# The last third of a modulation projection: its 16 weight tiles issued whole in the second mixer's norm

## The chip, the cores and the metric

The kernel runs on one core of one Trainium2 chip. The metric is the device time of one execution in microseconds (us), as the median of several runs.

## The reference

The program computes two blocks, one after the other, in float32. The first has two hybrid layers on 256 tokens of width 1024. A layer is a mixer and a feed-forward:

```
h = rms_norm(x, g_mix);  z = h @ w_in
o_a = mla_mixer(...);  o_b = conv_mixer(...);  o_c = nsa_mixer(...)
x = x + (g_a * o_a + g_b * o_b + g_c * o_c) @ w_out
h = rms_norm(x, g_ffn)
x = x + jnp.square(jax.nn.relu(h @ w_ff1)) @ w_ff2
```

The second block attends from the first one's result, with a context of 256 further tokens. Its norms are modulated: six vectors of 1024 for the tokens and six for the context come from two condition vectors, as `silu(c) @ w_mod + b_mod`, so `w_mod` is 1024 x 6144. Two of its parts are a differential attention and a recurrence over the tokens (wkv, a state of 64 x 64 for each of 16 heads); the recurrence runs over the context first.

## The kernel before, in words

TensorE (PE) does every product. Weights come from HBM by SP's queue, in pieces of up to 512 KB ("raw", four buffers), and each piece is split in two parts, wh by ScalarE (ACT, line 312) and wl by VectorE (DVE, line 277), three buffers each, because a float32 product is made of three passes: lines 333 to 335 or 351 to 353. PE works its instructions in the order in which they were issued, and so does SP's queue. A scheduler fixes that order when the program is built. It goes by the order of the code, by priorities, and by waits on named instructions, so a step that is written elsewhere moves others with it.

In a layer, `mixer` (line 473) norms the tokens, multiplies by w_in in units (tm0 to tm3, then four u2 units for the convolution, and more), runs the three mixers and their merges (oa, ob, oc), and ends with the output projection wo, eight matmul groups of 512 columns. `ffn` (line 888) norms again (`normT`, line 403: squares on ACT, a reciprocal root on DVE, xn scaled by both at lines 415 and 416, 16 transposes on PE at line 424, split into hh and hl at lines 394 and 395) and runs 16 blocks of f1 and f2.

Beside this the program computes pieces of the second block early. `mods_stream` (line 1017) makes the modulation vectors in three thirds of eight units. A unit loads two tiles of 128 x 1024 (line 1034, into one of four buffers named TG) and makes four matmuls of 32 x 512 from them (line 1035, two to a tile). At the end of a third come four transposes (line 1042) and additions. `mods_units(n, after)` (line 1012) issues the next n units; with `after` they are held behind a named matmul, `self.last`, the last of the stage before. The first third and three units of the second are issued in the first layer. The second mixer's norm issues five units, its end three more (before the last part of wo), and the norm of the second feed-forward five.

The four TG buffers also hold the gates that the mixer stored, the first weights of a compression (line 558) and, in `ffn`, constants and a weight for the recurrence (lines 900 to 903 and 1555). In `ffn(1)` the recurrence over the context (`wkv_front`, `wkv_back`) is issued with high priority beside f1 and f2, and its state S is stored at line 907. Its steps are lines 1376 (state times keys), 1392 and 1404 on PE, with VectorE between them. The second block starts by loading S.

Of the kernel before, what the change touches and what calls it, by code (L numbers as in the profile page):

```python
# [194 lines left out]
class Kern:  # L195
# [277 lines left out]
    def mixer(self, l, pool):  # L473
# [11 lines left out]
        hl = self.t(self.work, [128, 8, T], "hl", F32R)  # L485
        self.normT(self.halves(self.x), P["g_mix"], hh, hl, spare="t", hold=True)
        if l:
            self.mods_units(5, self.last)

        if l == 0:  # L490
            nc.sync.dma_start(self.consts, self.A["cst"])
# [253 lines left out]
        with self.stream("n"):  # L745
# [41 lines left out]
            for i0 in range(0, 4, 2):  # L787
# [9 lines left out]
                for j in range(2):  # L797
                    i = i0 + j
# [81 lines left out]
        with self.stream("t"):  # L880
            pw = [self.bank_pair(), [self.score_bank(), self.score_bank()]]
        for i in range(4):
            if i == 3:
                self.mods_units(3)
            self.linB_acc(f"wo{i}_{l}", pw, mh[:, 2 * i:2 * i + 2], ml[:, 2 * i:2 * i + 2], i == 0, i == 3)
        self.add_x(pw)

    def ffn(self, l, pool):

        nc = self.nc  # L890
        hh = self.t(self.work, [128, 8, T], "hh", F32R)
        hl = self.t(self.work, [128, 8, T], "hl", F32R)
        self.normT(self.halves(self.x), self.P["g_ffn"], hh, hl, spare="t")
        self.mods_units(5, self.last)
        self.spare_bank = False
        if l == 0:
            self.ctx_proj(pool)
        with self.stream("n", "c"), self.tc.high_priority(offset=30000):
            self.n4, self.n8 = 5, 6
            tg = self.t(pool, [128, D], "TG", bufs=4)  # L900
            self.wkv_consts(pool, tg[:, T:T + 264])
            wa = tg[:, :T]
            nc.sync.dma_start(wa, self.wad)
            S = self.t(pool, [128, 2, 4, 64], "S")
            nc.gpsimd.memset(S, 0.0)
            self.wkv_back(self.wkv_front(pool, 0, l, self.zc, wa), S)
            nc.sync.dma_start(self.Sd[l], S)
        with self.stream("t"):
            pw = [self.bank_pair(), [self.score_bank(), self.score_bank()]]
        prev = None  # L910
        for i in range(17):
            cur = None
            if i == 14 and l == 0:
                self.mods_units(3)
            if i < 16:
                for ps in self.linA_unit(f"f1{i}_{l}", hh, hl, 8):
                    r = self.t(pool, [128, 2, T], "mt", bufs=4)
                    nc.scalar.activation(r, ps, AF.Relu)
                    fh = self.t(pool, [128, 2, T], "OT", F32R, bufs=2)
                    fl_ = self.t(pool, [128, 2, T], "OL", F32R, bufs=2)  # L920
                    nc.scalar.activation(fh, r, AF.Square)
                    self.mul(r, r, r)
                    self.sub(fl_, r, fh.bitcast(F32))
                    cur = (fh, fl_)
            if i == 15 and l:
                self.ctx_front = [self.t(self.work, [128, 8, T], n, F32R) for n in ("hh", "hl")]
                for n in range(2):
                    nc.sync.dma_start(self.ctx_front[n].bitcast(F32), self.hcd[:, n])
            if prev:
                self.linB_acc(f"f2{i - 1}_{l}", pw, *prev, i == 1, i == 16)  # L930
            prev = cur
        self.spare_bank = True
        self.add_x(pw)
# [1019 lines left out]
```

## Time and profile before

| what | value |
|---|---|
| median of 3 runs | 2797.48 us (2794.47 to 2798.41) |
| the profiled execution | 2798.71 us, its span 2796.9 us |
| mean granted clock of TensorE | 0.946 of full speed |
| busy PE, weight loads, DVE, ACT | 2635.9, 2293.4, 1978.4, 1423.3 us |
| chain that ended last, by engine | PE 79%, DVE 10%, DMA 6%, ACT 4% |

Times of the profile are counted from the span's start. Busy time is the sum of instructions on an engine; the chain is followed back from the last instruction to whatever released each step. A row of a timeline gives the start, the length, the engine, the line, and what is computed from what (`m<-TG,cs` is a PSUM tile m from the weights TG and the condition cs), how many equal ones follow each other, and in brackets the idle time before it with what ended it. The records of a matmul overlap with the next one's, so prices are read from starts. Most tiles give four records; a few are missing.

### The profile page before, as it was taken

Reading aid. Unit: us, or ns where it says so; the run is one execution under the profiler, and the core shown is the slowest. Engines: PE = TensorE matmul, PEld = TensorE weight load, DVE = VectorE, ACT = ScalarE, POOL = GpSimd, SP = SyncE. Lnnn points to the kernel's source line nnn. Section 1 sums busy time; section 2 is a strip of 40 time slices with the busy share of each in tenths; the row PEclk is TensorE's granted clock in tenths of the full one; section 3 lists DMA queues with packets and bytes.
Section 4 is the critical chain, followed back from the end, with each engine's and each line's share of the span. In section 5 each row is a group of like instructions: output and inputs, shape, how many; then the busy total and the mean of one; then the engine's idle time right before and its main releaser. Section 6 shows DMA issues by size and latency. Waiting matters only on the chain.

```text
span 2796.9 us, 54976 instructions
## 1 busy us (share of the span) xinstructions
PE 2635.9 (94%) x21856; PEld 2293.4 (82%) x21856; DVE 1978.4 (71%) x4085; ACT 1423.3 (51%) x2392; POOL 14.2 (1%) x45
## 2 busy tenths in 40 slices
PE   7999899999999999987998979989989999999999
PEld 7986588886997768877888755779989998888887
DVE  5996668765897658766788776566987765666665
ACT  4554446543555446534664655444446554444444
POOL 0000000000000000000000000000000000000000
PEclk9999999999999999988999976699999999999999
DMA  5532866546543555535746522264664346666665
GB/s 189 175 124 88 263 225 199 168 152 219 167 147 126 162 199 170 173 107 166 237 134 200 166 68 59 67 200 163 190 185 137 122 149 208 215 208 219 207 216 183
DMA packets 212433, 472.00 MB, mean 169 GB/s; under 512 B 52816, under 2 KB 86480, under 8 KB 211152
## 3 DMA queue, kind: packets, MB, share of 16 engines
q1 hardware_dynamic: 212176, 468.48, 52.4%
q8 instruction: 172, 2.82, 0.4%
q14 instruction: 85, 0.70, 0.1%
HBM read 427.77 MB, written 40.63 MB: 167 GB/s over the span
## 4 chain that ended last, share of the span: by engine, by line
PE 79%; DVE 10%; DMA 6%; ACT 4%; issue 2%; SPq 0%; DVEq 0%; ACTq 0%
PE a L333 8%; PE a L335 8%; PE a L334 8%; PE b L353 4%; PE b L351 4%; PE b L352 4%; PE b L1767 3%; PE x L335 3%; PE x L333 3%; PE x L334 3%; PE a L352 3%; PE a L351 3%; PE a L353 3%; DVE wl L277 3%; DMA raw<-in_peer 2%
## 5 line engine op out<-in xcount | busy, mean ns | idle before, releaser
L312 ACT ACTIVATE wh<-raw 128x1024 fp32r<-128x1024 f32 (+1 forms) x701 | 638.2, 913 | 689.3 <-PE a L334 247.4
L277 DVE TENSOR_TENSOR wl<-raw,wh 128x1024 fp32r<-128x1024 f32 (+1 forms) x701 | 727.4, 1041 | 357.9 <-ACT wh L312 332.6
L333 PE MATMUL a<-hh,wh 128*128 128x256 f32 x1920 | 550.2, 287 | 8.8 <-ACT hh L1621 4.1
L335 PE MATMUL a<-hh,wl 128*128 128x256 f32 x1920 | 549.5, 286 | 4.5 <-DVE wl L277 4.2
L334 PE MATMUL a<-hl,wh 128*128 128x256 f32 x1920 | 547.2, 285 | 0.6 <-DVE hl L277 0.5
L333 PEld LDWEIGHTS a<-hh,wh 128*128 128x128 f32 x1920 | 365.5, 190 | 22.0 <-ACT wh L312 4.9
L335 PEld LDWEIGHTS a<-hh,wl 128*128 128x128 f32 x1920 | 365.2, 190 | 14.8 <-DVE wl L277 9.0
L334 PEld LDWEIGHTS a<-hl,wh 128*128 128x128 f32 x1920 | 364.9, 190 | 5.4 <-DVE hl L277 0.7
L333 PE MATMUL x<-hh,wh 128*128 128x256 f32 x720 | 205.8, 286 | 5.6 <-ACT wh L312 5.2
L335 PE MATMUL x<-hh,wl 128*128 128x256 f32 x720 | 206.6, 287 | 3.0 <-DVE wl L277 3.0
L334 PE MATMUL x<-hl,wh 128*128 128x256 f32 x720 | 204.9, 285 | 0.0
L352 PE MATMUL b<-wl,ah 128*128 128x512 f32 x512 | 201.0, 393 | 0.0
L351 PE MATMUL b<-wh,ah 128*128 128x512 f32 x512 | 191.2, 393 | 2.8 <-issue 2.8
L353 PE MATMUL b<-wh,al 128*128 128x512 f32 x512 | 191.8, 391 | 0.0
L333 PEld LDWEIGHTS x<-hh,wh 128*128 128x128 f32 x720 | 137.2, 191 | 9.0 <-ACT wh L312 6.7
L335 PEld LDWEIGHTS x<-hh,wl 128*128 128x128 f32 x720 | 136.9, 190 | 5.7 <-DVE wl L277 4.4
L1802 ACT ACTIVATE ah<-pact 128x256 fp32r<-128x256 f32 x128 | 52.6, 412 | 173.1 <-PE b L352 160.3
L334 PEld LDWEIGHTS x<-hl,wh 128*128 128x128 f32 x720 | 137.1, 190 | 0.8
L352 PE MATMUL a<-wl,hh 128*128 128x256 f32 (+2 forms) x416 | 128.6, 309 | 8.0 <-DVE wl L277 7.9
L351 PE MATMUL a<-wh,hh 128*128 128x256 f32 (+2 forms) x416 | 125.3, 308 | 6.2 <-DVE hl L395 3.9
L277 DVE TENSOR_TENSOR wl<-rawv,wh 128x1024 fp32r<-128x1024 f32 x84 | 101.7, 1222 | 37.1 <-ACT wh L312 37.0
L353 PE MATMUL a<-wh,hl 128*128 128x256 f32 (+2 forms) x416 | 125.9, 304 | 0.0
(672 smaller groups left out, 5436.7 us busy)
## 6 DMA issues: line engine op xcount, KB each, us to landing
raw<-in_flat SPq DMA_DIRECT2D x289, 512.0 KB, 4.0
raw<-in_peer SPq DMA_DIRECT2D x172, 512.0 KB, 3.9
raw<-in_flat SPq DMA_DIRECT2D x228, 256.0 KB, 3.6
rawv<-in_peer SPq DMA_DIRECT2D x84, 512.0 KB, 4.6
TG<-in_flat SPq DMA_DIRECT2D x52, 512.0 KB, 5.9
parked<-act SPq DMA_DIRECT2D x89, 128.0 KB, 2.1
pact<-parked SPq DMA_DIRECT2D x89, 128.0 KB, 4.5
w<-vtd SPq DMA_DIRECT2D x32, 128.0 KB, 4.1
```

The lines of the kernel that those rows point to most:

```text
L277: self.nc.vector.tensor_tensor(out, a, b, op=ALU.subtract)
L312: self.nc.scalar.activation(h, src, AF.Copy)
L333: mm(ps, wh[:, k], xh[:, k], start=first and k == 0, stop=False)
L334: mm(ps, wh[:, k], xl[:, k], start=False, stop=False)
L335: mm(ps, wl[:, k], xh[:, k], start=False, stop=last and k == nk - 1)
L351: mm(ps, xh[:, k], wh[:, k], start=first and k == 0, stop=False)
L352: mm(ps, xh[:, k], wl[:, k], start=False, stop=False)
L353: self.last = mm(ps, xl[:, k], wh[:, k], start=False, stop=last and k == nk - 1)
L1767: nc.tensor.matmul(ps[:, c], a[:, n, g, :, c], b[:, g, :, c], start=n == 0, stop=n == 2)
L1802: nc.scalar.activation(ah, act, AF.Copy)
```

## The change

The second mixer's norm now issues 13 units: the five that are left of the second third and all eight of the last. The mixer's end and the norm of the feed-forward issue none in the second layer; the first layer is as before. Line numbers from 895 on rise by one.

```diff
--- before.py
+++ after.py
@@ -485,7 +485,7 @@
         hl = self.t(self.work, [128, 8, T], "hl", F32R)
         self.normT(self.halves(self.x), P["g_mix"], hh, hl, spare="t", hold=True)
         if l:
-            self.mods_units(5, self.last)
+            self.mods_units(13, self.last)
 
         if l == 0:
             nc.sync.dma_start(self.consts, self.A["cst"])
@@ -880,7 +880,7 @@
         with self.stream("t"):
             pw = [self.bank_pair(), [self.score_bank(), self.score_bank()]]
         for i in range(4):
-            if i == 3:
+            if i == 3 and l == 0:
                 self.mods_units(3)
             self.linB_acc(f"wo{i}_{l}", pw, mh[:, 2 * i:2 * i + 2], ml[:, 2 * i:2 * i + 2], i == 0, i == 3)
         self.add_x(pw)
@@ -891,7 +891,8 @@
         hh = self.t(self.work, [128, 8, T], "hh", F32R)
         hl = self.t(self.work, [128, 8, T], "hl", F32R)
         self.normT(self.halves(self.x), self.P["g_ffn"], hh, hl, spare="t")
-        self.mods_units(5, self.last)
+        if l == 0:
+            self.mods_units(5, self.last)
         self.spare_bank = False
         if l == 0:
             self.ctx_proj(pool)
```

Three places of PE's order show what moves. The first is the second mixer, at the end of tm2 (184 columns) and the start of tm3 (256 columns). Before:

```order
L351 MATMUL a_7705<-wh_7714,hh_7449 128x184
L352 MATMUL a_7705<-wl_7715,hh_7449 128x184
L353 MATMUL a_7705<-wh_7714,hl_7450 128x184
L351 MATMUL a_7820<-wh_7823,hh_7449 128x256
L352 MATMUL a_7820<-wl_7824,hh_7449 128x256
L353 MATMUL a_7820<-wh_7823,hl_7450 128x256
L351 MATMUL a_7820<-wh_7823,hh_7449 128x256
```

After (`m_7579` is the last third's PSUM tile, `TG_...` its weight tiles):

```order
L351 MATMUL a_7781<-wh_7790,hh_7449 128x184
L1036 MATMUL m_7579<-TG_7580,cs_579_3460 32x512 x2
L1036 MATMUL m_7579<-TG_7584,cs_579_3460 32x512 x2
L1036 MATMUL m_7579<-TG_7588,cs_579_3460 32x512 x2
L352 MATMUL a_7781<-wl_7791,hh_7449 128x184
L353 MATMUL a_7781<-wh_7790,hl_7450 128x184
L351 MATMUL a_7896<-wh_7899,hh_7449 128x256
L352 MATMUL a_7896<-wl_7900,hh_7449 128x256
L1036 MATMUL m_7579<-TG_7592,cs_579_3460 32x512 x2
L353 MATMUL a_7896<-wh_7899,hl_7450 128x256
L351 MATMUL a_7896<-wh_7899,hh_7449 128x256
```

Three tiles stand together in tm2; the other 13 follow singly, the first here in tm3, the last in the fourth u2 unit. Before, none of the last third stands there.

The second place is the norm of the second feed-forward: the last matmuls of wo, the transposes of line 424 and the first of f1. Before:

```order
L424 MATMUL a_10939<-ident_61,xn_10898 128x128
L424 MATMUL a_10948<-ident_61,xn_10898 128x128
L1035 MATMUL m_10827<-TG_10995,cs_579_3460 32x512 x2
L424 MATMUL x_10957<-ident_61,xn_10898 128x128
L424 MATMUL a_10966<-ident_61,xn_10898 128x128
L1035 MATMUL m_10827<-TG_10999,cs_579_3460 32x512 x2
L424 MATMUL a_10939<-ident_61,xn_10898 128x128 x3
L424 MATMUL a_10948<-ident_61,xn_10898 128x128 x3
L424 MATMUL x_10957<-ident_61,xn_10898 128x128 x3
L424 MATMUL a_10966<-ident_61,xn_10898 128x128 x3
L1035 MATMUL m_10827<-TG_11003,cs_579_3460 32x512 x2
L333 MATMUL a_12161<-hh_10896,wh_12157 128x256
```

After:

```order
L353 MATMUL s_10794<-wh_10911,hl_10782 128x512
L424 MATMUL a_10990<-ident_61,xn_10949 128x128
L424 MATMUL a_10999<-ident_61,xn_10949 128x128
L424 MATMUL x_11008<-ident_61,xn_10949 128x128
L424 MATMUL a_11017<-ident_61,xn_10949 128x128
L424 MATMUL a_10990<-ident_61,xn_10949 128x128 x3
L424 MATMUL a_10999<-ident_61,xn_10949 128x128 x3
L424 MATMUL x_11008<-ident_61,xn_10949 128x128 x3
L424 MATMUL a_11017<-ident_61,xn_10949 128x128 x3
L333 MATMUL a_12161<-hh_10947,wh_12157 128x256
L334 MATMUL a_12161<-hl_10948,wh_12157 128x256
L335 MATMUL a_12161<-hh_10947,wl_12158 128x256
```

Before, eight tiles stand between wo and f1, the last three of them here, among the transposes; six more stand in wo and two in f1. After, the transposes follow wo's last matmul directly, and f1 follows the transposes.

The third place is the end of the second feed-forward, where the recurrence is left alone on PE: from the last f2 matmul (line 353) on, the first rows of each step's parts. Before:

```order
L353 MATMUL s_12154<-wh_13795,OL_13743 128x512
L1392 MATMUL x_11920<-w_1795_11436,w_1779_11199 32x64
...
L1404 MATMUL m_11939<-w_1795_11436,w_1761_11109 64x64 x8
...
L1376 MATMUL m_11961<-S_11038,w_1763_11111 32x64
...
L1392 MATMUL m_11983<-w_1795_11436,w_1779_11199 32x64
...
L1404 MATMUL x_12002<-w_1795_11436,w_1761_11109 64x64 x8
...
L1376 MATMUL x_12024<-S_11038,w_1763_11111 32x64
...
L1392 MATMUL x_12046<-w_1795_11436,w_1779_11199 32x64
...
L1404 MATMUL m_12065<-w_1795_11436,w_1761_11109 64x64 x8
...
L1376 MATMUL m_12087<-S_11038,w_1763_11111 32x64
...
L1392 MATMUL m_12109<-w_1795_11436,w_1779_11199 32x64
...
L1404 MATMUL x_12128<-w_1795_11436,w_1761_11109 64x64 x8
```

After:

```order
L353 MATMUL s_12154<-wh_13795,OL_13743 128x512
L1393 MATMUL m_11983<-w_1795_11436,w_1779_11199 32x64
...
L1405 MATMUL x_12002<-w_1795_11436,w_1761_11109 64x64 x8
...
L1377 MATMUL x_12024<-S_11038,w_1763_11111 32x64
...
L1393 MATMUL x_12046<-w_1795_11436,w_1779_11199 32x64
...
L1405 MATMUL m_12065<-w_1795_11436,w_1761_11109 64x64 x8
...
L1377 MATMUL m_12087<-S_11038,w_1763_11111 32x64
...
L1393 MATMUL m_12109<-w_1795_11436,w_1779_11199 32x64
...
L1405 MATMUL x_12128<-w_1795_11436,w_1761_11109 64x64 x8
...
L351 MATMUL x_13873<-wh_13876,hh_13747 128x256
```

Line 1376 (now 1377) begins a step. Before, three full steps follow the last f2 matmul, after it two; the third stands among the f2 matmuls in front.

## Rows read from the trace of the kernel before

**Rows 1.** The page: the span, and each engine's busy time.

```profile
span 2796.9 us, 54976 instructions
...
PE 2635.9 (94%) x21856; PEld 2293.4 (82%) x21856; DVE 1978.4 (71%) x4085; ACT 1423.3 (51%) x2392; POOL 14.2 (1%) x45
```

**Rows 2.** Instructions of line 1035, 900 to 1100 us: times of one in ns, starts.

```profile
L1035 PE MATMUL m<-TG,cs x64: 592/617/1062, 963.7 to 1011.2; 128*32 128x512 f32 x64
```

**Rows 3.** PE's timeline, second mixer's tm0 and tm1: start, us, engine, line, what.

```profile
682.14 0.28 PE L352 MATMUL a<-wl,hh 128*128 128x256 f32 x1
...
682.35 1.05 PE L1035 MATMUL m<-TG,cs 128*32 128x512 f32 x4
...
683.55 0.28 PE L351 MATMUL a<-wh,hh 128*128 128x256 f32 x1
...
698.63 1.05 PE L1035 MATMUL m<-TG,cs 128*32 128x512 f32 x4
```

**Rows 4.** PE's timeline, second mixer's wo, from its first matmul to its last.

```profile
959.91 0.40 PE L351 MATMUL a<-wh,hh 128*128 128x512 f32 x1
...
962.48 0.39 PE L353 MATMUL s<-wh,hl 128*128 128x512 f32 x1
...
980.31 1.91 PE L1035 MATMUL m<-TG,cs 128*32 128x512 f32 x12
...
988.80 0.39 PE L353 MATMUL s<-wh,hl 128*128 128x512 f32 x1
```

**Rows 5.** Waits, 680 to 740 us: who waited for whom, us, times, longest.

```profile
PE m L1035 <- DMA TG<-in_flat: 1.7, 2, 1.0
```

**Rows 6.** Instructions of line 1034, 660 to 700 us: issue to landing.

```profile
DMA to landing us min/median/max: 4.9/6.7/9.0
```

**Rows 7.** Waits, 740 to 780 us, all engines.

```profile
PE x L352 <- DVE wl L277: 1.9, 1, 1.9
```

**Rows 8.** PE's timeline, norm of the second feed-forward; idle time before in brackets.

```profile
996.02 1.92 PE L1035 MATMUL m<-TG,cs 128*32 128x512 f32 x4 [1.90 <-DMA TG<-in_flat]
...
1002.32 0.88 PE L424 MATMUL a<-ident,xn 128*128 128x128 f32 x6
...
1004.98 0.38 PE L333 MATMUL a<-hh,wh 128*128 128x256 f32 x1
```

**Rows 9.** ACT's timeline, the same norm.

```profile
995.15 0.72 ACT L416 ACTIVATE xn<-x,rs_y 128x512 f32<-128x512 f32 x1 [0.64 <-DVE rs_y L289]
...
1002.91 0.84 ACT L394 ACTIVATE hh<-a,pk 128x256 fp32r<-128x256 f32 x2 [7.04 <-PE a L424]
```

**Rows 10.** Windows: length, busy us of PE, PEld, DVE, ACT, POOL, clock, DMA, GB/s.

```profile
995.00:1000.00 5.00, 3.98 (x10) 0.66 (x10) 0.54 (x2) 0.72 (x1) 0.00 (x0) 0.50 1.01 347
```

**Rows 11.** PE's timeline, end of the second feed-forward and start of the next stage.

```profile
1234.70 1.08 PE L1392 MATMUL x<-w,w 32*32 32x64 f32 x32
...
1249.27 1.95 PE L1392 MATMUL x<-w,w 32*32 32x64 f32 x32 [1.38 <-DVE w L274]
...
1257.24 1.94 PE L1392 MATMUL m<-w,w 32*32 32x64 f32 x32 [1.39 <-DVE w L274]
...
1272.81 0.58 PE L351 MATMUL x<-wh,hh 128*128 128x256 f32 x1 [11.22 <-ACT wh L312]
...
1274.13 0.41 PE L351 MATMUL x<-wh,hh 128*128 128x256 f32 x1
...
1277.97 0.40 PE L351 MATMUL x<-wh,hh 128*128 128x256 f32 x1
```

**Rows 12.** POOL's timeline, 940 to 1010 us.

```profile
1002.46 0.32 POOL L1555 MEMSET TG<- 128x264 f32 x1 [65.62 <-PE m L1035]
```

**Rows 13.** Windows of lines 1392, 1404 and 1376 alone, one step inside ffn1.

```profile
1215.00:1232.00 17.00, 1.08 (x32) 0.92 (x32) 1.00 0.41 153
...
1215.00:1232.00 17.00, 0.70 (x32) 0.56 (x32) 1.00 0.41 153
...
1215.00:1232.00 17.00, 0.65 (x32) 0.49 (x32) 1.00 0.41 153
```

## The prediction

> **What bounds the kernel now.** I read the page first: TensorE is busy for 2635.9 of 2796.9 us [rows 1], so the question is where PE gains or loses time. The profiled execution took 2798.71 us, 1.81 us more than its span and 1.23 us over the median of 2797.48. The sum below is made against 2798.71 and then carried to the median. About 0.2%, 5.6 us, is what a measurement of this kernel can tell from no change.
>
> Next the instructions of the modulation's matmul line between 900 and 1100 us: they are the last third, 64 records for 16 weight tiles of 512 KB, two matmuls to a tile, 963.7 to 1011.2 us [rows 2]. Six tiles run inside the output projection wo of the second mixer, eight in the feed-forward's norm, two in f1. For each of the three places, and for the place they go to, I read PE's timeline.
>
> **The change part by part.**
>
> *Added to the second mixer.* By the order, three tiles stand together near the end of tm2 and 13 single ones between 256-column matmuls through tm3 and the four u2 units. What a single one costs there is shown by the second third's: from the matmul before it to the second one behind it took 683.55 - 682.14 = 1.41 us [rows 3], where two pitches of 0.115 would be 0.23, so a tile costs 1.18 us. The two matmuls of a tile run side by side, for the record of both lasts 1.05 us. Three together cost about 2.0 (the 1.91 us record in wo [rows 4] and a tenth for the change of shape). Sum: 13 x 1.18 + 2.0 = 17.3 us. The four transposes and the additions that close the third move along from f1 and cancel. Low end 15.6 (1.05 each). High end: the loads. Of the last eight tiles of the second third, up to 698.63 [rows 3], two held PE for 1.7 us together, the longer for 1.0 [rows 5], and landing took up to 9.0 us [rows 6]; the same share of 13 would be 2.8 more, 20.1. I take none, because the ring of buffers leaves these loads more time than the longest landing (worked out at the third rival). Against the 17.3, between 740 and 780 us PE stood 1.9 us waiting for one split weight from DVE [rows 7]; later work on PE can fill that. Between 0 and 1.9 I take 1.0. **Net +16.3.**
>
> The 16 loads also move on SP's queue, ahead of raw weights of the u2 units, and a load that waits for one of the four TG buffers holds the raw loads behind it. The compress weights use the same buffers and now come after. I cost this at nothing, because up to four raw tiles and three split ones are kept ahead of PE; if that cover goes, it is the third rival.
>
> *Removed from wo.* From the first wo matmul to the last of its 96 pass 28.89 us; 95 pitches of 0.2336 (959.91 to 962.48 in 11 steps [rows 4]) are 22.2. **-6.7**, with ends at -6.0 and -7.2 for the pitch's rounding.
>
> *Removed from f1.* Two singles at the price above: 2 x 1.18. **-2.4.**
>
> *The feed-forward's norm.* PE ends wo at 988.80 + 0.39 = 989.2 [rows 4] and begins f1 at 1004.98; eight tiles run in between, one of them at 996.02 after 1.90 us of waiting for its load [rows 8], and PE works in order, so the norm's transposes stand behind such tiles. The last quarter of xn is written by 995.15 + 0.72 = 995.87; yet hh follows only at 1002.91, after 7.04 us of waiting for transposes [rows 9]. With the tiles gone, only transposes stand there. From the six transposes at 1002.32 [rows 8] to hh is 0.59 us, and hh takes some 0.47, so f1 could begin at 995.87 + 0.59 + 0.47 = 996.9, 8.1 us sooner. But it then begins with a slow clock. Already with the tiles there, 995 to 1000 ran at a granted 0.50 (1.2 GHz) [rows 10]. Where PE comes back from a quiet stretch elsewhere, at 1272.81, the 18 steps from 1274.13 to 1277.97 have a pitch of 0.213 [rows 11], nearly twice the 0.115 above, and full rate follows: 5.2 us at about half rate lose 2.4. So 8.1 - 2.4: **-5.7**. Ends: -8.1 if the clock holds; -2.5 if f1's first evacuations take three us longer than I think.
>
> Here the Trainium skill speaks against the change. Its page "TensorE: Matmul & The Clock Gate", section "Part 1: The HAM clock gate", says that the array is throttled by default and that activity releases the throttle; the tiles were activity in this very gap. The trace agrees in direction, with 0.50 after the gap's waits [rows 10], but shows that the thin filler did not keep the clock. By the rule taken alone the term would be the -5.7 above; without it, -8.1.
>
> *The wkv chain at the end of ffn1.* Its constants take a TG buffer: POOL's memset sat 65.62 us until a modulation matmul released one, at 1002.46 [rows 12]. After the change that buffer is free before wo, and the order lets the first wkv matmuls run in the merges and wo. What this is worth shows at the end of the layer. After the last f2 matmul nothing but the recurrent chain runs: a step repeats every 1257.24 - 1249.27 = 7.97 us at half clock, and the next stage starts at 1272.81 [rows 11], after the state is stored. The new order has exactly one step fewer behind the last f2 matmul (two full ones instead of three). That removes 7.97 us there, but the step's matmuls now stand inside ffn1, where PE is full: busy 1.08 + 0.70 + 0.65 = 2.4 us [rows 13], 2.8 with the 0.13 that a change of shape costs at a single tile. **-5.2**; ends 0, if the chain arrives late and PE waits for it among f2, and -8.0, if its matmuls fill holes. The moved wkv front itself is as long as before and only changes which full stage it stands in: nothing, and if a load of its inputs is late, PE's whole queue in wo stands behind it.
>
> *Sum.* 16.3 - 6.7 - 2.4 - 5.7 - 5.2 = -3.7 us: 2795.0 against the profiled 2798.71, **2793.8** against the median. The tiles themselves cost more in the mixer than they free in wo and f1 (17.3 against 9.1), since the eight in the norm lay in a gap; what pays for it is a shorter gap and one step of the chain.
>
> **The rivals.**
>
> *The gap and the chain give all they hold.* The clock holds over the shorter gap (-8.1), the step's matmuls cost nothing (-8.0) and DVE's hole is filled (-1.9): 17.3 - 1.9 - 6.7 - 2.4 - 8.1 - 8.0 = -9.8, 2787.7. For it: the chain starts some 65 us sooner [rows 12]. Against: the 0.50 of the granted clock [rows 10], and full PE slices in ffn1.
>
> *The norm stays as long as it is.* The tiles were then mere filler in a gap that evacuations set: the term falls from -5.7 to 0, sum +2.0, 2799.5. For it: eight tiles fit there nearly free today. Against: 7.04 us between xn and hh in which only tiles and transposes ran [rows 9].
>
> *Slower: the moved loads starve the second mixer.* Each of the 13 singles waits as the two that waited did [rows 5], 0.7 to 1.0 us: 9.1 to 13.0 more, sum +5.4 to +9.3, middle 2804.8. This decides when a tile lands later than the ring gives it: landing took 4.9 to 9.0 us [rows 6], and by the order the singles stand 7 to 32 matmuls apart, the closest four neighbours 62 matmuls together: 62 x 0.115 + 4 x 1.18 = 11.8 us for the ring of four. So landing would have to grow by 2.8 us over the longest seen, or a raw load in front of a tile's load would have to wait that long on SP. Against: that margin, and six of the eight tiles before that did not wait.
>
> *The change does not do what it says:* the order would have to be bent by something at run time, above all the chain's step stalling PE instead of hiding: sum +1.5, 2799.0.
>
> **How the numbers follow.** My forecast has 0.46 (own range 2789 to 2799, from the ends of the norm and the chain), the full gain 0.24, the unchanged norm 0.12, starvation 0.15, the last 0.03. Faster by over 5.6 us: most of the second case (0.21) and a bit over a quarter of the first (0.14): 0.35. Slower by as much: most of starvation (0.13) and a sixth of the unchanged norm (0.02): 0.15. The rest, 0.50, is within. The range 2786 to 2803 leaves out the far part of the full gain and most of starvation, 0.2 together.
>
> **What would show it.** In the changed profile the modulation's matmuls should end in the u2 units near 750 us, with few waits for TG; wo should take 22 to 23 us; f1 should begin 7 to 9 us after wo's last matmul, its first matmuls at half rate; POOL's memset should come before wo; and the stretch from the chain's first matmul behind f2 to the next stage should shrink from 38.1 us (1234.70 to 1272.81 [rows 11]) to about 30. The prediction is wrong if waits for TG or for split weights in the u2 units come to more than 3 us, if f1 begins as late as before, or if f2 shows waits at the chain's matmuls.

## The result: slower, and the profile after

| | median, us | range | runs |
|---|---|---|---|
| before | 2795.72 | 2789.48 to 2798.41 | 5 |
| the change | 2812.34 | 2808.56 to 2823.19 | 5 |

The ratio is 1.0076, 95% interval 1.0052 to 1.0099. The change is 0.76% slower, some 17 us; 2793.8 was predicted, in a range that ended at 2803.

The page of the changed kernel, its first lines:

```profile
span 2810.6 us, 54973 instructions
...
PE 2647.1 (94%) x21856; PEld 2301.9 (82%) x21856; DVE 1981.7 (71%) x4085; ACT 1423.0 (51%) x2392; POOL 13.9 (0%) x45
```

Against [rows 1] the span is 13.6 us longer, and PE is busy 11.2 us more.

To see where, both traces are laid side by side by the matmuls of lines 333 to 335 and 351 to 353. There are 13344 in each kernel, so the n-th in one answers to the n-th in the other. The table gives the time between the same ones, in us. The first two columns are two profiles of before (the second is the first run below), then two of the change, then the spread of four profiles whose first block has the change's order (the two of the change, and those of reorder_1 and reorder_2 below).

| stretch | before | before | change | change | four profiles |
|---|---|---|---|---|---|
| second mixer's norm, tm0, tm1 | 39.9 | 39.1 | 37.8 | 39.5 | 37.8 to 39.5 |
| tm2, tm3, u2 and what follows | 123.8 | 123.8 | 145.0 | 143.2 | 143.2 to 145.0 |
| attention | 110.7 | 109.2 | 112.2 | 112.2 | 112.2 |
| merges | 20.0 | 19.8 | 25.9 | 25.8 | 25.8 to 25.9 |
| wo | 28.9 | 28.9 | 23.9 | 23.9 | 23.9 |
| norm of the feed-forward | 16.2 | 13.3 | 9.9 | 9.9 | 9.9 |
| f1 and f2 | 229.4 | 229.4 | 225.9 | 225.7 | 225.5 to 225.9 |
| last f2 to next stage | 38.4 | 38.8 | 31.0 | 30.6 | 30.6 to 31.0 |
| **sum of these** | 607.2 | 602.1 | 611.4 | 610.6 | 610.6 to 611.4 |
| second block: attention beside the recurrence | 214.6 | 208.8 | 221.0 | 219.9 | 216.9 to 231.7 |

So the stretch that the prediction added up lost 6.3 us on average, where it forecast a gain of 3.7, and 9 us more were lost in a stage that it did not look at. The rest of the 19.4 us between the mean spans of these profiles is scattered over the program in pieces of one or two microseconds.

**The second mixer.** PE's timeline of the change, one single tile in tm3 with the matmuls about it:

```profile
714.38 0.28 PE L352 MATMUL a<-wl,hh 128*128 128x256 f32 x1
...
714.59 1.05 PE L1036 MATMUL m<-TG,cs 128*32 128x512 f32 x4
...
715.58 0.39 PE L353 MATMUL a<-wh,hl 128*128 128x256 f32 x1
...
715.80 0.29 PE L351 MATMUL a<-wh,hh 128*128 128x256 f32 x1
```

From the matmul before to the second one behind it are 1.42 us, the 1.41 of [rows 3]: the price of a tile was right. All 14 groups together cost 17.5 us, worked out in the same way (13 x 1.19 and 2.0 for the three together), against 17.3 in the prediction, and none waited for its load. The waits of the change, 740 to 800 us, name what is beyond that:

```profile
PE x L352 <- DVE wl L277: 2.6, 1, 2.6
```

The hole that DVE leaves was not filled: it grew from 1.9 us [rows 7] to 2.6. And the clock fell for short spells, which it did in neither profile of before in this stretch. Windows of 5 us (columns as in [rows 10], PE's clock is the third number from the end), first behind that wait in the second profile of before:

```profile
774.00:779.00 5.00, 4.60 (x39) 4.61 (x40) 5.00 (x5) 1.23 (x2) 0.00 (x0) 1.00 0.50 132
```

Then the change, behind the same wait and in an earlier spell:

```profile
798.00:803.00 5.00, 4.60 (x26) 4.61 (x27) 5.00 (x5) 0.07 (x1) 0.00 (x0) 0.66 0.46 134
...
772.00:777.00 5.00, 5.00 (x19) 3.61 (x17) 2.55 (x8) 2.68 (x5) 0.00 (x0) 0.67 0.27 93
```

1.00 there, 0.66 and 0.67 here. The early spell cost 1.6 us against the second profile of the change, which lacks it. The three other profiles with this order have one or two such spells in the stretch as well. The wait alone does not decide it: behind the same wait the clock fell in the second profile of the change (2.56 us) and in reorder_2 (2.33 us, then 0.66 over 793 to 798), but not in reorder_1 (2.33 us, then 1.00 over 791.7 to 796.7). And the early spells follow no wait of PE of over 0.3 us in the stretch. What starts them is open.

**The merges.** The front of the context recurrence now starts among them. PE's timeline:

```profile
965.75 0.28 PE L335 MATMUL x<-OT,wl 128*128 128x256 f32 x1
...
967.39 1.92 PE L1199 MATMUL m<-consts,w 128*128 128x2 f32 x16 [1.37 <-issue]
```

PE stood 1.37 us ahead of the front's first matmuls, and these took 1.92 us. Behind them the large matmuls run at half rate for some three microseconds: the granted clock is 0.50 from 970 to 973.

**The feed-forward's norm.** PE's timeline from the last matmul of wo to f1:

```profile
1013.04 0.39 PE L353 MATMUL s<-wh,hl 128*128 128x512 f32 x1
...
1018.51 0.69 PE L424 MATMUL a<-ident,xn 128*128 128x128 f32 x2 [5.08 <-DVE xn L415]
...
1022.89 0.58 PE L333 MATMUL a<-hh,wh 128*128 128x256 f32 x1 [0.20 <-DVE hl L395]
...
1024.13 0.41 PE L335 MATMUL a<-hh,wl 128*128 128x256 f32 x1
...
1024.66 0.28 PE L335 MATMUL a<-hh,wl 128*128 128x256 f32 x1
```

f1 starts 9.85 us behind wo's last matmul's start, where it was 16.18 [rows 4, 8] and 13.27 in the second profile of before. It runs at half rate until 1024.3. The windows of the change (columns as in [rows 10]) have the granted clock at 1.2 GHz (0.50) through the transposes and f1's first matmuls, and then near 2.4 (0.96):

```profile
1018.00:1024.00 6.00, 5.04 (x21) 4.24 (x22) 4.17 (x15) 4.25 (x9) 0.00 (x0) 0.50 0.30 104
1024.00:1030.00 6.00, 6.00 (x56) 5.69 (x56) 1.74 (x7) 1.54 (x2) 0.00 (x0) 0.96 0.01 1
```

The second profile of before shows why its norm was 2.9 us shorter than the first: there the clock held through the norm, with the tiles in it, while the waits for the tiles' loads came to 3.7 us in both. Its window at about the place of [rows 10]:

```profile
989.00:994.00 5.00, 4.05 (x19) 1.14 (x20) 0.98 (x5) 0.77 (x2) 0.16 (x1) 1.00 0.98 324
```

**The tail.** PE's timeline, the first matmuls of each step that is left alone:

```profile
1249.09 1.08 PE L1393 MATMUL m<-w,w 32*32 32x64 f32 x32
...
1256.12 1.95 PE L1393 MATMUL x<-w,w 32*32 32x64 f32 x32 [1.38 <-DVE w L274]
...
1264.09 1.94 PE L1393 MATMUL m<-w,w 32*32 32x64 f32 x32 [1.39 <-DVE w L274]
...
1279.76 0.58 PE L351 MATMUL x<-wh,hh 128*128 128x256 f32 x1 [11.32 <-DMA raw<-in_flat]
```

Three groups of line 1392 (now 1393) instead of four [rows 11], with 7.97 us between the last two, and the next stage 30.7 us behind the first instead of 38.1.

### The profile page after: what moved, and what is told of

Same layout as the page of the kernel before. It is cut to its first block, busy times and chain, and to the rows that moved or that the text cites. A ratio compares the mean times of both kernels' runs of the same rounds, so it can differ in the third digit from the quotient of the medians.

```text
span 2810.6 us, 54973 instructions
## 1 busy us (share of the span) xinstructions
PE 2647.1 (94%) x21856; PEld 2301.9 (82%) x21856; DVE 1981.7 (71%) x4085; ACT 1423.0 (51%) x2392; POOL 13.9 (0%) x45
## 4 chain that ended last, share of the span: by engine, by line
PE 81%; DVE 9%; DMA 4%; ACT 4%; issue 2%; SPq 0%; DVEq 0%; ACTq 0%
PE a L333 9%; PE a L335 8%; PE a L334 8%; PE b L351 4%; PE b L352 4%; PE b L353 4%; PE b L1768 3%; PE x L333 3%; PE x L335 3%; PE x L334 3%; PE a L352 3%; PE a L351 3%; PE a L353 3%; DVE wl L277 2%; DMA raw<-in_peer 2%
```

## The experiments

**Both kernels once more.** No edit.

> The kernel before, unchanged, profiled once more, to learn how much a stage varies from run to run. Theory A (the loss in the second block comes from the order that the scheduler made there): the attention stage beside the token recurrence, 1592 to 1797 us in the first profile of before, takes the same 205 us within 2. Rival B (run-to-run variation): it moves by 5 us or more. The stretch before the second mixer, where both kernels have the same order and the change came out 2.8 us later, should vary by about 3 us under both.

> The changed kernel, unchanged, profiled once more. Theory A: the same stage of the second block is again some 6 us longer than in before, and the merges of the second mixer again come out some 7 us later than the tiles alone explain. Rival B: one or both of these vanish.

One execution each: 2782.22 us for before, 2807.42 for the change. The table above has both profiles. The second mixer, the merges, wo, f1 and the tail repeat within 2 us in either kernel; the norm of before varies by 2.9. The second block's stage repeats within 1.1 us in the change and within 5.8 in before, so it varies more than theory A allowed, and rival B is not excluded by this pair alone. (The expectation's 205 us end one large matmul group earlier than the table's stage.) In the round of this and the next two experiments before took 2773.59 to 2805.29 us in 23 runs; its runs in the other rounds lie within that.

**The recurrence held behind wo.** In the changed kernel:

```diff
-        with self.stream("n", "c"), self.tc.high_priority(offset=30000):
+        with self.stream("n", "c"), self.tc.high_priority(offset=30000), self.behind(self.last if l else None):
```

> The change, but the context recurrence of the second feed-forward is held behind the last matmul of wo, so that its front cannot enter the merges; the 13 units stay in the second mixer's norm. Theory A (the early front of the recurrence costs the merges about 7 us, by a stall of 1.4 us at its first matmul, DVE and ACT work in front of the attention's tail, and a longer spell at 1.2 GHz, and gives back only 4 to 5 in f1): some 2 to 6 us faster than the change, because the front's first matmuls now lie in the norm's gap. The step of the chain stays hidden, so the tail stays at about 30 us. Rival C (the merges were slowed by the moved tiles or their loads, not by the front): no faster, and the merges stay late.

Median 2807.37 us, ratio to before 1.0043 (1.0023 to 1.0063), 5 us under the change. The interval overlaps that of the change (1.0052 to 1.0099), so the whole time alone shows no clear gain. The merges are back at 20.6 us, and wo takes 22.2. PE's timeline in the norm shows where the front went:

```profile
1000.12 1.84 PE L1199 MATMUL m<-consts,w 128*128 128x2 f32 x16
...
1006.69 1.98 PE L1208 MATMUL m<-ident,rs_yn 128*64 128x128 f32 x16
...
1011.16 0.60 PE L1215 MATMUL m<-ident,w 128*128 128x128 f32 x4
```

These matmuls stand between wo, the transposes and f1, and the norm takes 13.9 us instead of 9.9. The sum of the first block's stretches is 608.2 against 610.9 on average in the four profiles with the change's order. Theory A holds for the merges: the front's cost there was 5 to 6 us. Rival C falls, but attention stays at 112.2, so those 2 us are not the front's. The second block's stage took 228.0 us here.

**Paired tiles.** Both loads of a unit ahead of its four matmuls, the later tile's first:

```diff
-                for q in range(4):
-                    if q % 2 == 0:
-                        raw = self.t(self.lpool, [128, 1024], "TG", bufs=4)
-                        nc.sync.dma_start(raw, self.view(f"mod{r}{k}")[:, 512 * q:512 * q + 1024])
-                    nc.tensor.matmul(ps[32 * q:32 * q + 32], cs[:, k], raw[...
+                raws = []
+                for q in (0, 2):
+                    raw = self.t(self.lpool, [128, 1024], "TG", bufs=4)
+                    nc.sync.dma_start(raw, self.view(f"mod{r}{k}")[:, 512 * q:512 * q + 1024])
+                    raws.append(raw)
+                for q in (2, 3, 0, 1):
+                    nc.tensor.matmul(ps[32 * q:32 * q + 32], cs[:, k], raws[q // 2][...
```

> The change, but the two tiles of a unit are loaded first and their four matmuls issued together, the later tile's first, so that four 32-row matmuls run side by side, as eight records in 1.07 us did in the norm of before. Theory A (a single tile costs 1.18 us because it fills half of the columns): 13 singles and a triple become 8 pairs, 17.1 us become about 9.5, and the second third and the first layer's singles gain some 4 us each: 8 to 15 us faster than the change. Rival D (a pair waits for two loads, so that PE stands for DMA): the gain is eaten by waits for TG of over 5 us.

Median 2788.06 us, 24 us under the change and 0.9977 (0.9956 to 0.9999) of before. PE's timeline in the second mixer, one pair:

```profile
712.07 1.06 PE L1038 MATMUL m<-TG,cs 128*32 128x512 f32 x8
```

Eight records in 1.06 us, as long as four took. The stretch with tm2 and u2 took 136.5 us, 7.7 less than the mean of 144.2 in the four profiles. One of the last third's eight pairs stands ahead of the stretch; with the stretch before it, which holds the second third's tiles too, it is 173.5 against 182.6 us. The eight pairs of the last third cost 9.5 us without their waits, where the change's 14 groups cost 17.5. The waits of this kernel, 665 to 850 us, show the price that rival D named:

```profile
PE m L1038 <- DMA TG<-in_flat: 4.5, 3, 3.4
```

4.5 us, the longest of 3.4; in the change it was 3.3 over nearly the same stretch. D takes a small part. The gain is larger than the tiles give, and the rest lies in the second block: its stage took 208.9 us. The order of PE in the second block is here that of before: the traces differ in no more rows than two profiles of before do. In the change some 370 of 11758 matmuls stand elsewhere.

**Other orders in the second block.** One scratch tile allocated and set, in the first run ahead of the loop over the token keys, in the second six at the start of the second token front:

```diff
+        dz = self.smallt(2)
+        for _ in range(1):
+            nc.vector.memset(dz, 0.0)
```

> The change, with one small scratch tile allocated and set on VectorE in the second block. Every PE row of the first block and the first part of the second is that of the change; from the point where the kernel before and the change part in the second block, the scheduler makes a third order. Theory A (the 9 us lost in the attention stage beside the token recurrence are a matter of which order the scheduler lands on, not of the moved tiles themselves): the first block takes what it takes in the change within 2 us, and the stage that takes 209 to 215 us in before and 220 to 221 in the change takes another value, by 4 us or more. Rival B (something that the first block leaves behind makes that stage long): it stays at 219 to 222.

> The same with six scratch tiles, at the start of the second token front, and a fourth order from the same point. Theory A: the first block as in the change within 2 us; the stage differs again from 220 us, or from the other order's value, by 4 us or more. Rival B: 219 to 222 once more.

Medians 2813.95 us (ratio 1.0068, 1.0052 to 1.0085) and 2812.98 us (1.0083, 1.0058 to 1.0109). The first block is the change's within 1 us, and the stage takes 231.7 and 216.9 us. The first is 11 us off the change, as theory A wanted; the second is only 3 to 4 off the change but 15 off the first, which theory A allowed as well. Neither lies at the 219 to 222 of rival B. In the runs of the second the time went from 2797.18 to 2821.01 with one order, and its profile is that of the fastest run: a good part of the time is decided at run time, and one profile does not give an order's usual stage.

**Pairs in the other places.** The paired version with the recurrence held, and the kernel before with pairs alone:

> Paired tiles, and the context recurrence held behind wo. Theory A: the first block takes the gains of both: the u2 stretch 136 to 137 us as with pairs, the merges back at 20 to 21 us and the norm near 14, so some 2 to 4 us better than pairs up to the end of the first block. The second block is on another order than before (265 rows of PE differ) and may lose 5 to 19 us in the attention stage, as it did twice. Rival E (the two interact, the front in the norm's gap pushes f1): the first block no better than pairs.

> The kernel before with paired tiles only; the last third stays in wo, the norm and f1. If the pairing is the whole gain, the first block is 6 to 9 us shorter than in before (first layer, second third, and about 3 us in wo and f1), the tail stays at 38 us because three steps of the chain follow f2, and the moved tiles of the change bring nothing more. If the place matters too, the version with pairs in the changed place is shorter in the first block by some 5 us, most of it the tail. The second block's order differs from before by 266 rows.

Medians 2804.5 us (1.0027, 1.0010 to 1.0045) and 2808.04 us (1.0054, 1.0037 to 1.0071). The first block's sums are 603.7 and 603.4 us, against 599.3 and 600.5 for pairs alone in the changed place and 604.7 on average in before. In the first, the stretch with tm2 and u2 took 140.8 us, not the 136 to 137 expected, with three spells at a clock of 0.50 in it. So the gains of pairing and of holding the front did not add, as rival E had it, and the place is worth some 3.5 us once tiles are paired: with the old place the tail stays at 38.8 us. What sank both is the second block, on orders of their own: 229.3 and 230.1 us in the stage.

These runs cross the two things. The tiles moved with the order of before (pairs): 208.9 and, repeated below, 212.0 us. Not moved with another order (pairs in before): 230.1. Over all profiles, before's order gave 208.8 to 214.6 us (five profiles of four kernels, the last experiment's 212.4 among them) and other orders 216.9 to 231.7 (seven profiles of six kernels), whether the tiles were moved or not. Four of these come from one and the same chip and split in the same way: 208.8 and 208.9 (before, pairs) against 219.9 and 228.0 (the change, the front held). The windows of the stage, columns as in [rows 10], for before (first profile, then the second), pairs, the change, reorder_1, reorder_2, and pairs in before:

```profile
1592.00:1806.00 214.00, 183.66 (x2450) 130.47 (x2449) 139.94 (x344) 111.49 (x269) 1.11 (x2) 0.67 0.23 65
```

```profile
1581.00:1791.00 210.00, 179.97 (x2465) 127.04 (x2464) 141.39 (x347) 112.47 (x271) 1.11 (x2) 0.72 0.24 69
```

```profile
1579.00:1788.00 209.00, 175.87 (x2456) 124.18 (x2456) 140.86 (x346) 111.59 (x268) 1.11 (x2) 0.73 0.24 68
```

```profile
1599.00:1820.00 221.00, 185.65 (x2456) 128.76 (x2455) 140.92 (x345) 112.01 (x271) 1.11 (x2) 0.71 0.22 64
```

```profile
1590.00:1822.00 232.00, 199.91 (x2459) 138.29 (x2458) 142.27 (x347) 112.83 (x272) 1.11 (x2) 0.65 0.22 62
```

```profile
1587.00:1804.00 217.00, 180.52 (x2457) 125.61 (x2456) 140.31 (x347) 112.59 (x272) 1.11 (x2) 0.73 0.23 66
```

```profile
1583.00:1813.00 230.00, 192.39 (x2456) 133.50 (x2455) 142.43 (x347) 112.72 (x271) 1.11 (x2) 0.68 0.22 63
```

DVE and ACT do the same work in all of them; PE's busy time and its clock differ, from 0.73 to 0.65 of full speed. The clock alone does not explain the lengths: at like clocks the other orders are longer, 230 us at 0.68 (pairs in before) against 214 at 0.67 (before), and 221 at 0.71 (the change) against 210 at 0.72 (before). The order alone does not either: before's own two profiles are 5.8 us apart, at 0.67 and 0.72. So order and clock both take part. Length less busy time is 30 to 33 us in before's order and 35 to 38 in the others, save reorder_1 (32). What in the orders makes the stage longer is not settled.

**The better version again, and one more shift.** The second edit gives the first feed-forward's norm eight units instead of five:

```diff
-            self.mods_units(5, self.last)
+            self.mods_units(8, self.last)
...
-            if i == 14 and l == 0:
+            if False:
                 self.mods_units(3)
```

> The version with paired tiles in the changed place once more, beside the kernel before. If the gain over before is real, the ratio lies again between 0.995 and 1.000, the first block from tm2 to the next stage takes 599 to 603 us against 602 to 607 in before and 611 in the change, and the attention stage of the second block, whose order is row for row that of before, takes 208 to 215. If the first reading was luck of the runs, the ratio is at or above 1.000.

> Paired tiles, and the first layer's feed-forward norm issues eight units instead of five, with none left for its fifteenth block. The order puts five of the pairs into the end of the first feed-forward and seven of the last third's or second third's pairs fewer stand alone in the second mixer; the second block keeps the order of before. If a pair costs about 1.2 us wherever PE is full, nothing is gained over the other paired version (within 3 us); if waits for loads in the second mixer's norm were still a part, it is 2 to 5 us faster.

Pairs: 2786.06 us in 12 runs, 0.9978 (0.9962 to 0.9994), first block 600.5, stage 212.0. Both readings agree: it is faster than before by 0.2% and than the change by about 1%.

The other took 2913.93 us, 1.0440 (1.0415 to 1.0465), a miss of the whole expectation. POOL's timelines tell where, first of the second run of pairs, then of this run. The row is the start of the first layer's recurrence over the context:

```profile
424.59 0.16 POOL L1247 MEMSET lp<- 128x32 f32 x1 [85.61 <-ACT w L1279]
```

```profile
349.22 0.32 POOL L1558 MEMSET TG<- 128x264 f32 x1 [81.56 <-PE m L1038]
...
665.09 0.16 POOL L1247 MEMSET lp<- 128x32 f32 x1 [315.38 <-ACT w L1279]
```

It came 240 us later, behind the feed-forward instead of beside it, though its TG buffer was free at 349.22, in pairs at 338.49. PE's timeline of this run shows what stood ahead of it:

```profile
643.87 1.93 PE L1038 MATMUL m<-TG,cs 128*32 128x512 f32 x8 [3.26 <-DMA TG<-in_flat]
...
646.54 1.98 PE L1210 MATMUL m<-ident,rs_yn 128*64 128x128 f32 x16 [0.74 <-ACT mt L268]
```

The front's matmul into the PSUM tile m (line 1210) follows the last tile of the second third, and waits for ACT's copy of that third's sums (mt, line 268). There is one bank named m in the code (`pool("psm", bufs=1, ...)`): a third of the modulation holds it from its first unit to its copy, and the front of the recurrence needs it too. With eight units in the norm, the second third was opened there and closed only in the second mixer. No run with a second bank was made, so that the bank held the front is read from the order and not tested. Behind it the recurrence ran nearly alone, at half clock:

```profile
720.00:760.00 40.00, 11.12 (x190) 9.15 (x186) 22.05 (x51) 3.26 (x6) 0.00 (x0) 0.50 0.13 27
```

So the 65.62 us of POOL [rows 12] were read too narrowly: a TG buffer was late there, and by the order the bank m was not free either. In before, the front's first matmul into m stands at 1020.24, after the last third's transposes at 1015.58. Whether the bank or the buffer set the start there was not tried.

## Why the prediction was wrong

It named 2793.8 us; the change took 2812.34.

- **"What bounds" and the sum: the second block was left out.** The sum ended at the start of the next stage, as if nothing behind it moved. The step that failed is this silent zero. The scheduler's order parts from that of before deep in the second block, some 260 us behind that block's start (1273 to 1535 us in before), and the stage there was longer by 8.7 us on average (220.4 against 211.7, two profiles each). The runs show that this does not come from the tiles: with the tiles moved and before's order it was 208.9 and 212.0, with the tiles in place and another order 230.1. The order takes part at either clock, as every profile with another order is longer than every one with before's; it does not set the length alone, as this varies within one order too. What in the order costs the time stays open.
- **"Net +16.3" for the second mixer: 20.4 (mean of the four profiles).** The price of a tile held (17.5 us for all against 17.3). Wrong were the two ends of the term. The 1.0 us that a hole of DVE was to give back became 0.7 us more of waiting, and spells at 1.2 GHz came on top. The rival of starved loads did not happen: no single tile waited.
- **"The moved wkv front ... nothing": 6.0 us in the merges, and 1.7 in wo.** wo fell by 5.0 instead of 6.7, and by just 6.7 with the front held. f1 and f2 gave back 3.7, of which -2.4 for two tiles and +2.8 for a step were foreseen, so some 4 belong to the front. That a stage is full does not make work equal in every stage: here the front brought a stall of 1.37 us and a spell at half clock with it. Attention, which the sum left out as well, took 112.2 us against 109.2 and 110.7; why is not known.
- **The norm, -5.7.** It measured -6.3 against the profile that the prediction used and -3.4 against the second one. f1 began later than I worked out (9.85 us behind wo's last matmul, where 8.1 had been reckoned as start), since all 16 transposes stand ahead of it at half rate; and less was lost at f1's start. The granted clock was 0.50 from 1018 to 1024 and 0.96 in the six microseconds behind. The rule of the Trainium skill's page "TensorE: Matmul & The Clock Gate", section "Part 1: The HAM clock gate", that the array is throttled unless activity releases it, agrees with these two numbers. The prediction also read from [rows 10] that the tiles in the gap did not keep the clock. That was one execution: in the second profile of before they did (1.00 in the window shown above), and there the gap left only 3.4 us to win.
- **The tail, -7.97 and +2.8 inside ffn1.** The first part is right to 0.2 us (-7.8). The second cannot be told apart from the effect of the front that left f1.
- **The place.** The first block lost 6.3 us where -3.7 was forecast. In the rivals' terms none was it: the norm shrank, the loads came in time.

Of the 19.4 us between the profiles (17 between the medians) 6.3 are thus placed in the first block, stage by stage, and 8.7 in one stage of the second. The rest is scatter that this study cannot place.

## What to carry to other kernels

Where a scheduler sets the order, a change's sum has to run to the program's end: compare the order of every later stage, and when one parts, treat its length as unknown by the spread that such a stage shows. Before moving work between full stages, ask what shape it has: narrow matmuls that leave columns empty are cheaper made side by side (17.5 us became about 9.5, waits apart) than moved. And look at who else needs the buffer or the PSUM bank that the moved work holds while it is open.

## What was unexpected

- Two tiles' matmuls in one go took 1.06 us, and one tile's 1.05: the second tile was free wherever both had landed.
- A wait of 2.6 us in a stretch where PE was otherwise full was followed by 5 us at a mean clock of 0.66; the same wait of 1.9 us in before was followed by 5 us at 1.00. Between the two it went either way: 2.33 us kept the clock in reorder_1 and lost it in reorder_2.
- One and the same kernel, before, ran from 2773.59 to 2805.29 us in 23 runs, 1.1%; between its two profiles the stage in the second block varied most of the stretches in the table, by 5.8 us.
